# A pooling mixer computed on rounded high and low parts instead of plain fp32

## The chip, the cores and the metric

One core of one Trainium2 chip runs the whole network as one program. The metric is the device time of one execution in microseconds, of the slowest (here the only) core; lower is better.

## The reference, cut to what matters

The program is a stack of four mixers and feed-forward layers on 512 tokens of width 1024. The change touches the first mixer alone, a causal moving average minus the token itself, over four groups of 256 channels with windows of 2, 4, 8 and 16, followed by one 256 by 256 matrix for each group:

```python
h = rms_norm(x, norm_mix[0])
for g, win in enumerate((2, 4, 8, 16)):
    c = cs[:, :, g]                      # cumulative sum over tokens
    lag = jnp.pad(c[:, :-win], ((0, 0), (win, 0), (0, 0)))
    mean = (c - lag) / jnp.minimum(n_avail, float(win))[:, None]
    outs.append(mean - hf[:, :, g])
p = jnp.stack(outs, axis=2)
y = jnp.einsum('bsgc,gcd->bsgd', p, w).reshape(B, S, D)
x = x + y * scale
h = rms_norm(x, norm_ffn[0])             # then x = x + swiglu(h, ...)
```

## The kernel before

**How matrices are multiplied.** The network's accuracy is kept with two kinds of product on TensorE. Nearly everywhere an fp32 operand is split into a high part, rounded to the engine's fp32r format by a ScalarE copy, and a low part, the difference, taken by VectorE or GpSimd. `mm3` then multiplies high by high, high by low and low by high, three fp32r passes. `hilo` splits a tile, `hilo_g` (line 521) splits a tile times a per-partition gain, both with one ScalarE and one VectorE instruction. The pooling mixer alone uses plain fp32 matmuls, which the trace shows as two passes each.

**The pooling mixer** (`pool_mixer`, line 627). `x` is held transposed, channels on partitions, as eight tiles of 128 by 512. Because the pooling is linear, the group's matrix is applied first and the pooling after. `gains` multiplies the pool weights by the norm's gain. `squares` makes the sum of squares of the eight tiles of `x` (ScalarE squares, VectorE adds), has TensorE sum it over partitions (`col_sums`), and turns it into `rcol`, the reciprocal root mean square of each token (a VectorE step and a GpSimd power). `products` multiplies, for each group `g` and each half `jj` of the tokens, two token blocks `j` with two channel blocks `k` into one PSUM bank. `evac` reads that bank, multiplies by `rcol` and writes the tile `z`; a bank holds two halves of 256 columns, and each half has its own `rcol` column, so each half is an instruction of its own: ScalarE takes the first, VectorE the second. Then, for each of eight tiles `d`, `products` multiplies `z` by a banded matrix `bands[g]` (the moving average minus identity), and `finish` adds the result to `x` (VectorE), splits the new `x` into `xh` and `xl` (ScalarE, VectorE), squares it (ScalarE) and adds the square to `ss` (GpSimd).

**What follows.** The first feed-forward layer (`ffn`) starts each accumulation with `xh[0]`, `xl[0]` and goes to `xh[7]`, `xl[7]`; its TensorE queue runs on without a gap that matters. Its weights come through `Stream`: a raw tile of 2048 columns is loaded by SyncE's queue and split in four parts; `pump` issues one part (ScalarE's high part; the low part goes to VectorE and GpSimd in turn). The mixer's task `weights` pumps the first eight parts while the mixer runs.

**What sets the order.** Each engine works through its instructions in program order. The order is made while the kernel is built: tasks are generators, `Sched.run` steps the ready one with the lowest rank (then the one that has waited longest), and `Plan` keeps a price-based clock for each engine that says when a yielded tile will be there. `get` and `put` hand out PSUM banks: four named `acc`, two `t`, two `s`. The times of the plan fix nothing but the order. A tile's dependencies are turned into semaphore waits by the framework.

Of the kernel before, what the change touches and what calls it, by code (L numbers as in the profile page):

```python
# [9 lines left out]
F32R = mybir.dt.float32r  # L10
BF = mybir.dt.bfloat16
I32 = mybir.dt.int32
AF = mybir.ActivationFunctionType
OP = mybir.AluOpType
# [3 lines left out]
P = 128  # L18
# [3 lines left out]
KT = D // P  # L22
# [431 lines left out]
class Net:  # L454
# [37 lines left out]
    def mm(self, ps, lhsT, rhs, start=True, stop=True):  # L492
        self.nc.tensor.matmul(ps, lhsT, rhs, start=start, stop=stop)
# [133 lines left out]
    def pool_mixer(self):  # L627

        nc, a, sched = self.nc, self.a, self.sched
        self.ss = {}  # L630
        pw, bands, zs = [], [], {}
        for g in range(4):
            w = self.tmp("pw")
            nc.sync.dma_start(out=w, in_=a["pool_w"][:, g])
            nc.dma(0.73, w)
            pw.append(w)
            x = self.x[:, 2 * g:2 * g + 2]
            nc.sync.dma_start(out=x, in_=a["xT"][:, 2 * g:2 * g + 2])
            nc.dma(1.46, self.x[:, 2 * g], self.x[:, 2 * g + 1])
        for g in range(4):  # L640
            b = self.tmp("bnd")
            nc.sync.dma_start(out=b[:, :384], in_=a["bands"][:, g])
            nc.dma(0.55, b)
            bands.append(b)
        self.constants()
        self.ws.load()
        self.rcol = None
        self.new_norm("ffn0")

        def gains(g):  # L650
            yield pw[g]
            for k in range(2):
                c = slice(k * 256, (k + 1) * 256)
                nc.vector.tensor_scalar(pw[g][:, c], pw[g][:, c], self.vec("mix0", 2 * g + k),
                                        None, op0=OP.mult)

        def squares():
            for d in range(KT):
                yield self.x[:, d]
                q = self.tmp("sq")  # L660
                nc.scalar.activation(q, self.x[:, d], AF.Square)
                if d == 0:
                    self.ss["x"] = q
                else:
                    yield q
                    nc.vector.tensor_tensor(self.ss["x"], self.ss["x"], q, op=OP.add)
            ps = yield from self.get("t")
            yield self.ss["x"]
            self.col_sums("x", ps)
            self.rcol = False  # L670
            yield ps
            r = self.rstd(ps[:, :NT], D, "rcol")
            self.put("t")
            yield r
            self.rcol = r

        def evac(g, jj, tag, ps):
            while not self.rcol:
                yield 0.1
            yield ps  # L680
            z = self.tmp("z")
            for j in range(2):
                o = slice(j * 256, (j + 1) * 256)
                r = self.rcol[:, 2 * jj + j:2 * jj + j + 1]
                if j:
                    nc.vector.tensor_scalar(z[:, o], ps[:, o], r, None, op0=OP.mult)
                else:
                    nc.scalar.activation(z[:, o], ps[:, o], AF.Copy, scale=r)
            self.put(tag)
            yield z  # L690
            zs[g, jj] = z

        def finish(d, ps):
            nc.vector.scalar_tensor_tensor(self.x[:, d], ps, self.vec("pscale", d),
                                           self.x[:, d], op0=OP.mult, op1=OP.add)
            self.put("acc")
            yield self.x[:, d]
            self.xh[d], self.xl[d] = self.tmp("xh", F32R), self.tmp("xl", F32R)
            yield from self.split(self.xh[d], self.xl[d], self.x[:, d], self.vec("ffn0", d))
            self.square_sum("x", self.x[:, d], "x" not in self.ss, eng=nc.gpsimd)  # L700

        def products():
            for g in range(4):
                for jj in range(2):
                    tag = "acc" if g < 2 else "s" if g == 2 else "t"
                    if g == 2:
                        yield from self.wait("rcol")
                    ps = yield from self.get(tag)
                    yield pw[g], self.x[:, 2 * g], self.x[:, 2 * g + 1]
                    for j in (2 * jj, 2 * jj + 1):  # L710
                        for k in range(2):
                            self.mm(ps[:, (j % 2) * 256:(j % 2 + 1) * 256],
                                    self.x[:, 2 * g + k, j * P:(j + 1) * P],
                                    pw[g][:, k * 256:(k + 1) * 256], start=(k == 0),
                                    stop=(k == 1))
                    sched.spawn(evac(g, jj, tag, ps), 1, ps)
                    yield 0.0
            for d in range(KT):
                g, hd = d // 2, d % 2
                while (g, 0) not in zs or (g, 1) not in zs:  # L720
                    yield 0.1
                ps = yield from self.get("acc")
                yield bands[g]

                def mm(j, rhs, c0, c1, start=False, stop=False):
                    o = (j % 2) * 256 + hd * P
                    self.mm(ps[:, c0:c1], zs[g, j // 2][:, o:o + P], rhs, start, stop)

                b = bands[g]
                mm(0, b[:, 256:384], 0, 128, start=True)  # L730
                mm(0, b[:, 128:256], 128, 256)
                mm(2, b[:, 0:256], 256, 512)
                mm(1, b[:, 0:256], 128, 384)
                mm(3, b[:, 0:128], 384, 512, stop=True)
                sched.spawn(finish(d, ps), 1, ps)
                yield 0.0

        def weights():
            yield 14.0
            for i in range(8):  # L740
                self.ws.pump()
                yield 0.7

        for g in range(4):
            sched.spawn(gains(g), 0)
        sched.spawn(squares(), 1)
        sched.spawn(products(), 2)
        sched.spawn(weights(), 0)


# [1329 lines left out]
def _host(inp):  # L2080

    f = np.ascontiguousarray
    o = {}
# [33 lines left out]
    for name, w in (("mla_o", inp["mla_w_o"]), ("da_o", inp["da_w_out_2"])):  # L2117
        w = w[0].reshape(KT, P, 4, 2, P)
# [17 lines left out]
    r = np.arange(P)  # L2136
# [4 lines left out]
    c = np.arange(T)[None, :] - 3 * P - r[:, None]  # L2141
# [7 lines left out]
    o["causal"] = np.where(r[None, :] > r[:, None], np.float32(-1e30), np.float32(0))  # L2149

    o["ident"] = np.eye(P, dtype=np.float32)
    b = np.zeros((P, 4, 384), np.float32)
    p, c = np.arange(P)[:, None], np.arange(256)[None, :]
    for g, w in enumerate(WINDOWS):
        inside = (c - p >= 0) & (c - p < w)
        b[:, g, :256] = inside * np.float32(1.0 / w) - (c == p)
        n = np.minimum(c[:, :P] + 1, w).astype(np.float32)
        b[:, g, 256:] = inside[:, :P] / n - (c == p)[:, :P]
    o["bands"] = b
    return o  # L2160

# [38 lines left out]
```

## Time and profile before

| | us |
|---|---|
| median of three runs | 1568.91 |
| lowest, highest | 1567.87, 1570.69 |
| the profiled execution | 1568.89 |
| its span, first to last instruction | 1567.1 |

The span is what the profile's rows add up to; 1.79 us of the profiled execution lie outside it. PE is TensorE's matmul row and PEld its weight loads, DVE is VectorE, ACT ScalarE, POOL GpSimd. The mixer takes the first 42 us of the span, and the rest is the feed-forward layers, two attention mixers and a mixture of experts.

### The profile page before, as it was taken

How to read it: one execution, taken by the hardware profiler on the slowest of the kernel's cores; microseconds unless marked ns; L12 is line 12 of the kernel's file. 1: busy time of each engine (PE TensorE's matmuls, PEld its weight loads, DVE VectorE, ACT ScalarE, POOL GpSimd, SP SyncE). 2: the span in 40 equal slices, each digit the busy share in tenths (PEclk: the TensorE clock that was granted, in tenths of full speed). 3: DMA queues.
4: the chain of work that ended last, by engine and by line, in shares of the span. 5: the costliest groups of instructions: out<-in, count | busy, mean ns of one | idle time of the engine just before them, and what ended most of it. 6: DMA issues, size and time to landing. Idle time of an engine off the chain costs nothing. (4 is left out here: it accounts for less than half of the span.)

```text
span 1567.1 us, 21562 instructions
## 1 busy us (share of the span) xinstructions
PE 1495.6 (95%) x7752; PEld 1233.7 (79%) x7752; DVE 1017.4 (65%) x1668; ACT 782.9 (50%) x1585; POOL 508.8 (32%) x382
## 2 busy tenths in 40 slices
PE   8999999999999999999999999999989699999996
PEld 7788888888878888888888889998978466666664
DVE  6564344445477754443444466988984699999996
ACT  5323222323366633332233345787783478787884
POOL 4322122311231113321232223322222466565553
PEclk9999999999999999999999999999989699999998
DMA  6121333223210223214322232211068889999961
GB/s 241 61 107 56 116 111 108 73 75 119 69 63 28 68 108 121 99 42 142 108 86 86 74 119 84 78 55 68 28 202 296 261 302 362 345 355 360 348 206 27
DMA packets 69935, 221.61 MB, mean 141 GB/s; under 512 B 7616, under 2 KB 16960, under 8 KB 56640
## 3 DMA queue, kind: packets, MB, share of 16 engines
q1 hardware_dynamic: 56448, 201.03, 35.9%
q0 software_dynamic: 4064, 14.16, 3.7%
q10 hardware_dynamic: 9312, 5.01, 1.1%
q8 instruction: 62, 1.02, 0.3%
q14 instruction: 49, 0.40, 0.1%
HBM read 208.63 MB, written 11.53 MB: 140 GB/s over the span
## 5 line engine op out<-in xcount | busy, mean ns | idle before, releaser
L341 POOL TENSOR_TENSOR lo<-raw,hi 128x512 fp32r<-128x512 f32 (+1 forms) x157 | 224.4, 1439 | 694.4 <-ACT hi L341 592.4
L341 PE MATMUL acc<-xh,hi 128*128 128x512 f32 x744 | 290.5, 390 | 0.3 <-ACT xh L341 0.3
L341 PE MATMUL acc<-xl,hi 128*128 128x512 f32 x744 | 289.6, 389 | 0.3 <-DVE xl L341 0.3
L341 PE MATMUL acc<-xh,lo 128*128 128x512 f32 x744 | 289.5, 389 | 0.0
L341 DVE TENSOR_TENSOR wl<-raw,wh 128x512 fp32r<-128x512 f32 x288 | 268.1, 982 | 6.1 <-ACT wh L341 5.7
L341 ACT ACTIVATE hi<-raw 128x512 fp32r<-128x512 f32 (+1 forms) x378 | 208.8, 607 | 86.1 <-issue 59.8
L341 DVE TENSOR_TENSOR lo<-raw,hi 128x512 fp32r<-128x512 f32 (+1 forms) x221 | 215.9, 987 | 19.6 <-ACT hi L341 18.9
L341 ACT ACTIVATE wh<-raw 128x512 fp32r<-128x512 f32 x384 | 211.8, 621 | 15.8 <-PE acc L341 10.0
L341 POOL TENSOR_TENSOR wl<-raw,wh 128x512 fp32r<-128x512 f32 x96 | 147.1, 1533 | 119.4 <-ACT wh L341 90.8
L341 PEld LDWEIGHTS acc<-xh,hi 128*128 128x128 f32 x744 | 139.7, 188 | 29.6 <-ACT xh L341 0.7
L341 PEld LDWEIGHTS acc<-xl,hi 128*128 128x128 f32 x744 | 139.7, 188 | 29.1 <-DVE xl L341 0.6
L341 PEld LDWEIGHTS acc<-xh,lo 128*128 128x128 f32 x744 | 139.6, 188 | 29.1
L341 DVE TENSOR_TENSOR u<-acc,R 128x512 f32<-128x512 f32 x44 | 30.4, 691 | 181.0 <-PE acc L341 181.0
L341 PE MATMUL acc<-hh,hi 128*128 128x512 f32 x352 | 136.9, 389 | 0.0
L341 PE MATMUL acc<-hl,hi 128*128 128x512 f32 x352 | 136.9, 389 | 0.0
L341 PE MATMUL acc<-hh,lo 128*128 128x512 f32 x352 | 136.9, 389 | 0.0
L341 ACT ACTIVATE hh<-t 128x512 fp32r<-128x512 f32 x44 | 27.8, 632 | 218.4 <-DVE t L341 218.4
L341 DVE TENSOR_TENSOR x<-acc,x 128x512 f32<-128x512 f32 x59 | 40.5, 690 | 121.0 <-PE acc L341 120.9
L341 PE MATMUL acc<-hi,xh 128*128 128x256 f32 x384 | 111.0, 289 | 0.0
L341 PE MATMUL acc<-lo,xh 128*128 128x256 f32 x384 | 108.7, 283 | 0.6 <-DVE lo L341 0.6
L341 PE MATMUL acc<-hi,xl 128*128 128x256 f32 x384 | 108.5, 283 | 0.0
L341 PE MATMUL acc<-wl,teh 128*96 128x512 f32 x256 | 102.5, 401 | 3.3 <-POOL wl L341 1.7
(314 smaller groups left out, 2917.9 us busy)
## 6 DMA issues: line engine op xcount, KB each, us to landing
raw<-moe_w SPq DMA_DIRECT2D x200, 256.0 KB, 7.1
raw<-moe_w SPq DMA_DIRECT2D x46, 1024.0 KB, 7.3
raw<-ffn_gu SPq DMA_DIRECT2D x43, 1024.0 KB, 4.8
raw<-ffn_dn SPq DMA_DIRECT2D x32, 704.0 KB, 4.0
raw<-da_in SPq DMA_DIRECT2D x12, 1024.0 KB, 4.7
raw<-mla_up SPq DMA_DIRECT2D x4, 832.0 KB, 4.4
raw<-mla_o_a SPq DMA_DIRECT2D x12, 256.0 KB, 4.3
raw<-da_o_a SPq DMA_DIRECT2D x12, 256.0 KB, 3.9
```

What stands on the lines that cost most here:

```text
L341: r = f(*args, **kw)
```

## The change

`x` and the gained pool weights are split into high and low parts, and the products are made of three fp32r passes instead of two fp32 ones. `z` is split as it leaves PSUM, by `hilo_g`, half by half. The bands are loaded raw into `bndr` tiles (400 columns instead of 384) and rounded into fp32r tiles by GpSimd copies. The band of the first token block is stored as a high part and, for its first 16 columns, a low part; the other bands hold one fp32r value. Each `d` then takes nine fp32r matmuls instead of five fp32 ones: `z` high and low against the band, and one matmul of 16 columns for the band's low part. `squares` moves from rank 1 to rank 0 and follows the splits of `x`; `weights` waits for the sum of squares to have been issued instead of for a fixed time.

```diff
+        xs, ws, raws = [None] * KT, [None] * 4, []
...
         for g in range(4):
-            b = self.tmp("bnd")
-            nc.sync.dma_start(out=b[:, :384], in_=a["bands"][:, g])
-            nc.dma(0.55, b)
-            bands.append(b)
+            t = self.tmp("bndr")
+            nc.sync.dma_start(out=t[:, :400], in_=a["bands"][:, g])
+            nc.dma(0.57, t)
+            raws.append(t)
...
         def gains(g):
             yield pw[g]
+            h = self.pair("pw")
             for k in range(2):
                 c = slice(k * 256, (k + 1) * 256)
-                nc.vector.tensor_scalar(pw[g][:, c], pw[g][:, c], self.vec("mix0", 2 * g + k),
-                                        None, op0=OP.mult)
+                self.hilo_g(h[0][:, c], h[1][:, c], pw[g][:, c], self.vec("mix0", 2 * g + k))
+            yield h
+            ws[g] = h
+
+        def rounded():
+            yield from self.wait("rcol")
+            for t in raws:
+                yield t
+                b = self.tmp("bnd", F32R)
+                nc.gpsimd.tensor_copy(b[:, :400], t[:, :400])
+                yield b
+                bands.append(b)
+
+        def parts():
+            for d in range(KT):
+                yield self.x[:, d]
+                h = self.pair("xp")
+                self.hilo(*h, self.x[:, d])
+                xs[d] = h
 
         def squares():
             for d in range(KT):
-                yield self.x[:, d]
+                while xs[d] is None:
+                    yield 0.1
                 q = self.tmp("sq")
                 nc.scalar.activation(q, self.x[:, d], AF.Square)
...
-            z = self.tmp("z")
+            z = self.pair("z")
             for j in range(2):
                 o = slice(j * 256, (j + 1) * 256)
                 r = self.rcol[:, 2 * jj + j:2 * jj + j + 1]
-                if j:
-                    nc.vector.tensor_scalar(z[:, o], ps[:, o], r, None, op0=OP.mult)
-                else:
-                    nc.scalar.activation(z[:, o], ps[:, o], AF.Copy, scale=r)
+                self.hilo_g(z[0][:, o], z[1][:, o], ps[:, o], r)
             self.put(tag)
...
-                            self.mm(ps[:, (j % 2) * 256:(j % 2 + 1) * 256],
-                                    self.x[:, 2 * g + k, j * P:(j + 1) * P],
-                                    pw[g][:, k * 256:(k + 1) * 256], start=(k == 0),
-                                    stop=(k == 1))
+                            xh, xl = (t[:, j * P:(j + 1) * P] for t in xs[2 * g + k])
+                            wh, wl = (t[:, k * 256:(k + 1) * 256] for t in ws[g])
+                            self.mm3(ps[:, (j % 2) * 256:(j % 2 + 1) * 256], xh, xl, wh, wl,
+                                     k == 0, k == 1)
...
-                mm(0, b[:, 256:384], 0, 128, start=True)
-                mm(0, b[:, 128:256], 128, 256)
-                mm(2, b[:, 0:256], 256, 512)
-                mm(1, b[:, 0:256], 128, 384)
-                mm(3, b[:, 0:128], 384, 512, stop=True)
+                v = "p (a b) -> p a b"
+                for n in range(2):
+                    self.mm(ps[:, 0:256].rearrange(v, b=P), zs[g, 0][n][:, hd * P:(hd + 1) * P],
+                            b.rearrange(v, b=P)[:, 0:3:2], n == 0, False)
+                mm(0, 0, b[:, 384:400], 0, 16)
+                for j, c in ((2, 256), (1, 128)):
+                    for n in range(2):
+                        mm(j, n, b[:, 128:384], c, c + 256)
+                for n in range(2):
+                    mm(3, n, b[:, 128:256], 384, 512, stop=(n == 1))
                 sched.spawn(finish(d, ps), 1, ps)
                 yield 0.0
 
         def weights():
-            yield 14.0
+            yield from self.wait("rcol")
             for i in range(8):
                 self.ws.pump()
                 yield 0.7
...
-        sched.spawn(squares(), 1)
+        sched.spawn(parts(), 0)
+        sched.spawn(rounded(), 0)
+        sched.spawn(squares(), 0)
```

`_host` lays the bands out in the new order and makes the low part of the first block.

## Rows read from the trace of the kernel before

**Rows 1.** The page's first part: busy us, share of the span, instructions.

```profile
PE 1495.6 (95%) x7752; PEld 1233.7 (79%) x7752; DVE 1017.4 (65%) x1668; ACT 782.9 (50%) x1585; POOL 508.8 (32%) x382
```

**Rows 2.** Busy time by stretch, with the granted clock, DMA share and GB/s last.

```profile
10.00:15.00 5.00, 5.00 (x21) 4.28 (x20) 3.90 (x8) 2.30 (x4) 0.00 (x0) 1.00 1.07 365
...
30.00:35.00 5.00, 5.00 (x36) 4.69 (x36) 5.00 (x7) 4.28 (x8) 4.84 (x4) 1.00 0.64 234
...
60.00:70.00 10.00, 10.00 (x46) 8.29 (x45) 7.51 (x10) 3.35 (x6) 3.04 (x3) 1.00 0.37 123
```

**Rows 3.** Timeline of TensorE's matmuls: start, length, instruction, idle time before it.

```profile
6.49 9.67 PE L341 MATMUL acc<-pw,x 128*128 128x256 f32 x32 [6.49 <-DMA x<-xT]
15.99 0.95 PE L341 MATMUL pst<-ones,sq 128*128 128x1 f32 x8
...
23.79 12.43 PE L341 MATMUL acc<-bnd,z 128*128 128x128 f32 x80
...
42.10 0.50 PE L341 MATMUL acc<-xl,hi 128*128 128x512 f32 x1 [0.28 <-DVE xl L341]
...
43.26 1.05 PE L341 MATMUL pst<-ones,ss 128*128 128x1 f32 x8 [0.42 <-POOL ss L341]
```

**Rows 4.** Timeline of VectorE, 4 to 64 us.

```profile
4.78 0.62 DVE L341 TENSOR_SCALAR pw<-pw,vecs 128x256 f32<-128x256 f32 x2 [4.78 <-DMA vecs<-vecs]
...
11.86 3.87 DVE L341 TENSOR_TENSOR sq<-sq 128x512 f32<-128x512 f32 x5
...
22.36 0.48 DVE L341 TENSOR_SCALAR z<-pss,rcol 128x256 f32<-128x256 f32 x1 [2.62 <-ACT z L341]
...
27.02 0.73 DVE L341 SCALAR_TENSOR_TENSOR x<-acc,vecs,x 128x512 f32<-128x512 f32 x1
27.67 0.71 DVE L341 TENSOR_TENSOR lo<-raw,hi 128x512 fp32r<-128x512 f32 x1
...
41.30 0.75 DVE L341 SCALAR_TENSOR_TENSOR xl<-x,vecs,xh 128x512 fp32r<-128x512 f32 x1 [0.79 <-ACT xh L341]
```

**Rows 5.** Timeline of ScalarE, 4 to 64 us.

```profile
6.38 1.15 ACT L341 ACTIVATE sq<-x 128x512 f32<-128x512 f32 x2 [3.92 <-DMA x<-xT]
...
18.32 1.67 ACT L341 ACTIVATE hi<-raw 128x512 fp32r<-128x512 f32 x3 [4.60 <-DMA raw<-ffn_gu]
21.86 0.47 ACT L341 ACTIVATE z<-pss,rcol 128x256 f32<-128x256 f32 x1 [1.87 <-POOL rcol L341]
```

**Rows 6.** Timeline of GpSimd: the second sum of squares ends, its power follows.

```profile
41.93 1.27 POOL L341 TENSOR_TENSOR ss<-ss,sq 128x512 f32<-128x512 f32 x1 [0.93 <-ACT sq L341]
44.59 1.03 POOL L341 TENSOR_TENSOR rcol<-rcolv,mhalf 128x4 f32<-128x4 f32 x1 [1.39 <-DVE rcolv L341]
```

**Rows 7.** Timelines of ScalarE and VectorE in the second attention, one PSUM bank split.

```profile
979.01 0.84 ACT L341 ACTIVATE v<-acc,r 128x256 fp32r<-128x256 f32 x2
...
979.88 0.88 DVE L341 SCALAR_TENSOR_TENSOR v<-acc,r,v 128x256 fp32r<-128x256 f32 x2 [1.87 <-PE pss L341]
```

**Rows 8.** Groups by form, 0 to 45 us: count, busy us, mean ns, idle before.

```profile
L341 POOL TENSOR_TENSOR ss<-ss,sq 128x512 f32<-128x512 f32 x7 | 11.1, 1582 | 1.3 <-ACT sq L341 0.9
...
L341 DVE SCALAR_TENSOR_TENSOR xl<-x,vecs,xh 128x512 fp32r<-128x512 f32 x8 | 8.7, 1098 | 0.8 <-ACT xh L341 0.8
...
L341 DVE SCALAR_TENSOR_TENSOR x<-acc,vecs,x 128x512 f32<-128x512 f32 x8 | 5.9, 739 | 0.0
```

**Rows 9.** Timeline of TensorE: the first and the seventeenth of a run of 256-column fp32r matmuls.

```profile
961.79 0.28 PE L341 MATMUL acc<-hi,xh 128*128 128x256 f32 x1
...
963.71 0.28 PE L341 MATMUL acc<-hi,xl 128*128 128x256 f32 x1
```

**Rows 10.** Busy time by stretch around a gap in TensorE's work; the clock stands third from last.

```profile
1128.00:1131.00 3.00, 1.39 (x11) 0.87 (x8) 2.06 (x4) 2.91 (x7) 0.12 (x1) 1.00 0.00 0
1131.00:1132.00 1.00, 0.33 (x1) 0.18 (x1) 0.55 (x1) 0.97 (x3) 0.00 (x0) 0.58 0.00 0
1132.00:1138.00 6.00, 5.80 (x26) 5.80 (x27) 3.16 (x15) 2.92 (x12) 0.00 (x0) 0.50 0.00 0
```

More of the change, by code (lines that the diff above doesn't have):

```diff
@@ L708, in products @@
                     ps = yield from self.get(tag)
-                    yield pw[g], self.x[:, 2 * g], self.x[:, 2 * g + 1]
+                    while ws[g] is None or xs[2 * g + 1] is None:
+                        yield 0.1
+                    yield xs[2 * g] + xs[2 * g + 1]
                     for j in (2 * jj, 2 * jj + 1):
                         for k in range(2):
-                            self.mm(ps[:, (j % 2) * 256:(j % 2 + 1) * 256],
-                                    self.x[:, 2 * g + k, j * P:(j + 1) * P],
-                                    pw[g][:, k * 256:(k + 1) * 256], start=(k == 0),
-                                    stop=(k == 1))
+                            xh, xl = (t[:, j * P:(j + 1) * P] for t in xs[2 * g + k])
+                            wh, wl = (t[:, k * 256:(k + 1) * 256] for t in ws[g])
+                            self.mm3(ps[:, (j % 2) * 256:(j % 2 + 1) * 256], xh, xl, wh, wl,
+                                     k == 0, k == 1)
                     sched.spawn(evac(g, jj, tag, ps), 1, ps)
@@ L721, in products, with mm @@
                     yield 0.1
+                while len(bands) <= g:
+                    yield 0.1
                 ps = yield from self.get("acc")
                 yield bands[g]
-                def mm(j, rhs, c0, c1, start=False, stop=False):
+                def mm(j, n, rhs, c0, c1, start=False, stop=False):
                     o = (j % 2) * 256 + hd * P
-                    self.mm(ps[:, c0:c1], zs[g, j // 2][:, o:o + P], rhs, start, stop)
+                    self.mm(ps[:, c0:c1], zs[g, j // 2][n][:, o:o + P], rhs, start, stop)
                 b = bands[g]
-                mm(0, b[:, 256:384], 0, 128, start=True)
-                mm(0, b[:, 128:256], 128, 256)
-                mm(2, b[:, 0:256], 256, 512)
-                mm(1, b[:, 0:256], 128, 384)
-                mm(3, b[:, 0:128], 384, 512, stop=True)
+                v = "p (a b) -> p a b"
[8 more added lines that the diff above has]
+                    mm(3, n, b[:, 128:256], 384, 512, stop=(n == 1))
                 sched.spawn(finish(d, ps), 1, ps)
@@ L2151, in _host @@
     o["ident"] = np.eye(P, dtype=np.float32)
-    b = np.zeros((P, 4, 384), np.float32)
+    b = np.zeros((P, 4, 400), np.float32)
     p, c = np.arange(P)[:, None], np.arange(256)[None, :]
@@ L2155, in _host @@
         inside = (c - p >= 0) & (c - p < w)
-        b[:, g, :256] = inside * np.float32(1.0 / w) - (c == p)
+        b[:, g, 128:384] = inside * np.float32(1.0 / w) - (c == p)
         n = np.minimum(c[:, :P] + 1, w).astype(np.float32)
-        b[:, g, 256:] = inside[:, :P] / n - (c == p)[:, :P]
+        b[:, g, :128] = inside[:, :P] / n - (c == p)[:, :P]
+    high = (b[:, :, :128].view(np.uint32) & np.uint32(0xFFFFE000)).view(np.float32)
+    b[:, :, 384:] = (b[:, :, :128] - high)[:, :, :16]
+    b[:, :, :128] = high
     o["bands"] = b
```

## The prediction

> **What bounds the kernel now.** I read the page first. TensorE is busy for 1495.6 of 1567.1 us [rows 1], so over the whole span it is the bound, and a change that takes matmul passes away looks good. That is an average. The table of busy time by stretch, read next, tells another story of the 42 us that the change touches. Between 10 and 15 us TensorE works without a gap and VectorE 3.90 of 5 us; between 30 and 35 us VectorE is at 5.00 of 5 and TensorE as well; from 60 us on TensorE is full and VectorE is not [rows 2]. So the reader should ask which of the two ends the mixer last.
>
> TensorE's timeline answers: products from 6.49, the sums over partitions at 15.99 to 16.94, the bands from 23.79 to 36.22. The feed-forward layer starts right behind, but stops for its last input: the matmul at 42.10 waits 0.28 us for `xl` [rows 3]. VectorE's timeline shows that wait's other end, `xl` of tile 7, from 41.30 to 42.05 [rows 4]. From `rcol` at 21.86 [rows 5] to there VectorE hardly rests. **The end of the mixer is the end of VectorE's queue**, and TensorE, in front of its last three matmuls of the first group, merely waits. Behind it TensorE is full again [rows 2], so what the mixer loses or gains there the whole program does, one for one.
>
> VectorE's 42.05 us split into three parts. The sum of squares is ready at 11.86 + 3.87 = 15.73 [rows 4]; `rcol` follows at 21.82, because its steps stand in line behind weight parts that waited for their transfer (18.32, [rows 5]). The `z` tiles take from there to 27.02, when the first `x` step starts: 5.2 us. Then come eight `x` steps, eight `xl` and a weight part, to 42.05: 15.0 us [rows 4].
>
> **Part 1, up to `rcol`.** The order on each engine I worked out by stepping the tasks through the planner's rules; it gives ScalarE gains 0, copies of x0 and x1, squares 0 and 1, gains 1 and 2, and so on, and VectorE the same with the low parts and the adds. The durations come from rows. A VectorE instruction lasts 0.73 us and the next starts 0.65 us after it (27.02 and 27.67, [rows 4]), so 0.08 us overlap. One add or low part of 512 columns therefore costs about 0.61 us (0.69 long: 3.87 us for five, with small waits). A scaled low part of 256 columns costs 0.40 us (0.88 us for two of 0.48, [rows 7]); the plain multiply that it replaces cost 0.31 (0.62 for two, [rows 4]).
>
> x0 lands at 6.38 [rows 5]. Its copy takes some 0.61 us (1.67 for three with overlap, [rows 5]), so VectorE starts on x at about 7.0. It then has 8 low parts of x and 7 adds at 0.61 and 6 low parts of the weights at 0.40: 9.2 + 2.4 = 11.6 us, where it used to have 7 adds and 6 multiplies. Three waits for ScalarE early on add about 1.1 us. The sum of squares is then ready at 19.7, 4.0 us later than before. With no waits it is 18.6; both ends stay in the range.
>
> From that sum to `rcol` nothing stands in the way now, since `weights` follows it in program order. The second norm shows the bare chain: sum ready at 41.93 + 1.27 = 43.20, power from 44.59 to 45.62, 2.4 us [rows 6]. So `rcol` comes at 22.2 against 21.82: **+0.4 us**. The move of `weights` thus gives back most of what the splits cost. It costs nothing itself while ScalarE rounds the first three parts before `rcol` anyway, the raw tile landing at 18.3 [rows 5].
>
> The band copies by GpSimd stand ahead of its first weight part and of the power in its order, but need only transfers that land by about 13 us, when GpSimd is idle (0.00 of 5 us, [rows 2]). No row shows a 400-column copy; bounded by nothing below and by a 512-column two-input step of 1.58 us [rows 8] above, four end before 20 us at the worst. I take no cost. The 4% longer transfer of the bands lies behind `x` in SyncE's queue and is hidden likewise.
>
> **Part 2, the `z` tiles.** Before, a tile took one instruction of ScalarE and one of VectorE. Now each half takes both, and the second reads the first's result. There are two prices, far apart.
>
> If ScalarE may run ahead, VectorE's 16 low parts at 0.40, with three weight parts among them at 0.61, take 6.4 + 1.8 = 8.2 us instead of 5.2.
>
> But both halves of a tile lie in one PSUM bank, and the rows show what the program does with two readers of a bank. At 21.86 ScalarE reads the first half of `pss`, to 22.33; VectorE, which needs nothing from that instruction and has had `rcol` as long, starts on the other half at 22.36, and the wait is named as ScalarE's [rows 4, 5]. In the second attention ScalarE writes two halves `v` back to back from 979.01 to 979.85; VectorE, idle for 1.87 us, needs only the first, which ended at about 979.48, yet starts at 979.88, 0.03 us after the second [rows 7]. The later reader of a bank waits for the earlier one. No row has VectorE first and ScalarE second, but the wait is made from program order, and I see no reason that it should hold one way only. The new order inside a tile is ScalarE, VectorE, ScalarE, VectorE, all on one bank. So the second high part waits for the first low part, and the engines take turns.
>
> One tile then goes: high part 0 to 0.47, low part 0.50 to 0.98, high part 1.01 to 1.48, low part 1.51 to 1.99. The next tile's high part may follow 0.37 us after the second one (0.84 for two, [rows 7]), at 1.38, but its low part waits for VectorE until 1.92, so a tile costs 1.42 us. Seven tiles and a last one of 1.92 give 11.9 us. Three weight parts stand between them in ScalarE's order, each pushing the next high part by about 0.6: 13.7 us from `rcol` to the first `x` step. That is **+8.5 us** over 5.2. Queued behind on VectorE are the `x` steps, all of them, since the planner issues the tiles as one block; TensorE and the accumulation banks wait for these.
>
> The Trainium skill, "PSUM — Partial Sum Buffer", section "PSUM bank collisions raise a hardware error", says that any two engines on one bank have to be kept apart, reads against reads included, whatever columns they touch. By that the second price holds in either order of the engines; the rows here show one order.
>
> **Part 3, from the first `x` step to the last `xl`.** The work is the same: eight steps of 0.74 and eight of 1.10 us mean, slowed while GpSimd adds squares [rows 8]. The order differs: four `x` steps come at once, with four banks ready, so tile 7's is no longer last but one, and the wait of 0.79 us for its `xh` [rows 4] goes: **-0.8 us**. Together: 0.4 + 8.5 - 0.8 = 8.1 us.
>
> **TensorE's side.** A 256-column fp32r matmul follows the last after 0.12 us (1.92 us for 16, [rows 9]). Behind the sums there are 48 matmuls of products and 72 of bands; those of 128 and 16 columns no row shows, and I take them at 0.12 too (between nothing and that). With 1.0 us for the sums that is 15.4 us; before, the same stretch ran from 15.99 to 36.22, 20.2 us [rows 3]. The 4.8 us won go nowhere, because TensorE waits for VectorE: four bands can run before the first `x` step gives a bank back, then there are some 5 us without work.
>
> Such gaps have a price of their own. After 3 us with 1.39 us of work, the granted clock fell at 1131 to 0.50, the lower level of 1.2 GHz, and stayed there for 6 us of full work [rows 10]. At half rate the four bands still open take 4 x 9 x 0.24 = 8.6 us and the first feed-forward group up to tile 6 some 9.6, in 14 us that are there for both; it just fits if the clock comes back in six, as it did. I add nothing, and up to 3 us in the range. The Trainium skill, "TensorE: Matmul & The Clock Gate", names the same thing as a hazard of gaps between bursts; this trace agrees (0.50 after the gap at 1131).
>
> **The sum** is made against the profiled execution, 1568.89 us, which lies 0.02 us from the median: 1568.9 + 8.1 = 1577.0 us.
>
> **The rivals.** *The halves do not take turns* (ScalarE runs ahead). Then part 2 costs 8.2 - 5.2 = +3.0 and the sum is 0.4 + 3.0 - 0.8 = +2.6: 1571.5 us. For it: no row has ScalarE waiting. Against: the two rows where VectorE does.
> *TensorE is the bound.* It was without a gap from 6.49 to 36.2. If VectorE and ScalarE kept up, bands would end at 19.7 + 0.1 + 15.4 = 35.2 instead of 36.2 and the program would gain 1.0 us: 1567.9 us, not slower. It decides only if VectorE's queue ends before about 41 us. Even without turns it ends near 44.7, so I give it little.
> *The clock decides.* If it stays at the lower level from the gap until past the first group of 24 matmuls, TensorE ends bands and group at about 36 + 8.6 + 24 x 0.455 = 55.5 instead of 50.8, 4.7 us on top: 1581.7 us. For it: TensorE's work is thin from 30 to 45. Against: at half rate it is full there, and full work brought the clock back [rows 10].
>
> **How the numbers follow.** Turns: 0.68, its own range 1574 to 1580.5 us (sum ready earlier, copies overlapping better; against that a lower clock for a while). No turns: 0.15. TensorE the bound: 0.06. The clock: 0.11. The range from 1571.5 to 1581.5 leaves out the last two. About 0.2% (3.1 us) is what a measurement of this kernel can tell from no change. No turns and the TensorE case fall mostly within it: same 0.15. Faster keeps 0.05 for a price of part 1 that I have too high together with TensorE as the bound; slower has 0.80.
>
> **What the profile after would show.** Right: on `z`, ScalarE and VectorE alternate with starts some 0.5 us apart, and ScalarE's idle time there names VectorE; the first `x` step starts near 36 us, the last `xl` ends near 50; TensorE has gaps between 28 and 38 us. Wrong: ScalarE's second half of a tile starts before VectorE's first has ended; `rcol` later than 24 us (VectorE's splits dearer) or earlier than 20; the mixer's shift not found again at the end of the program, which would mean that a later stage gives or takes something.

## The result and the profile after

| | before | after |
|---|---|---|
| median of four runs, us | 1569.8 | 1584.03 |
| lowest, highest | 1567.87, 1571.66 | 1580.68, 1585.0 |
| profiled execution; its span | 1568.89; 1567.1 | 1585.0; 1583.2 |

The changed kernel is slower: ratio 1.0087, 95% interval 1.0067 to 1.0107. That is 14.2 us by the medians and 16.1 us between the two profiled executions, where 8.1 us had been forecast; 1584.0 lies above the range's upper end of 1581.5. The direction was right, and so was the largest of its three terms; the size was not.

The page's first part of the kernel after answers to [rows 1]:

```profile
PE 1497.7 (95%) x7776; PEld 1236.4 (78%) x7776; DVE 1030.9 (65%) x1684; ACT 793.2 (50%) x1609; POOL 506.5 (32%) x386
```

TensorE's busy time hardly moved, although two fp32 passes became three fp32r ones; the next views show that part of it ran at half the clock. VectorE has 13.5 us more to do. Neither says where 16 us went, so the mixer is read stage by stage. ScalarE's timeline after:

```profile
4.86 1.28 ACT L341 ACT_TABLE_LOAD   x1 [4.86 <-DMA pw<-pool_w]
...
9.04 1.69 ACT L341 ACTIVATE pwh<-pw,vecs 128x256 fp32r<-128x256 f32 x4
...
15.61 2.17 ACT L341 ACTIVATE sq<-x 128x512 f32<-128x512 f32 x4
...
26.79 0.48 ACT L341 ACTIVATE zh<-pss,rcol 128x256 fp32r<-128x256 f32 x1 [6.41 <-PE pss L341]
...
29.23 0.84 ACT L341 ACTIVATE zh<-acc,rcol 128x256 fp32r<-128x256 f32 x2 [0.58 <-DVE zl L341]
30.65 0.84 ACT L341 ACTIVATE zh<-acc,rcol 128x256 fp32r<-128x256 f32 x2 [0.58 <-DVE zl L341]
```

VectorE's timeline after, to be held against [rows 4]:

```profile
7.61 1.29 DVE L341 TENSOR_TENSOR xpl<-x,xph 128x512 fp32r<-128x512 f32 x2
9.57 1.69 DVE L341 SCALAR_TENSOR_TENSOR pwl<-pw,vecs,pwh 128x256 fp32r<-128x256 f32 x4 [0.67 <-ACT pwh L341]
...
12.50 2.21 DVE L341 TENSOR_TENSOR xpl<-x,xph 128x512 fp32r<-128x512 f32 x3
14.63 1.39 DVE L341 SCALAR_TENSOR_TENSOR pwl<-pw,vecs,pwh 128x256 fp32r<-128x256 f32 x2
15.95 1.00 DVE L341 TENSOR_TENSOR sq<-sq 128x512 f32<-128x512 f32 x1
...
18.08 3.86 DVE L341 TENSOR_TENSOR sq<-sq 128x512 f32<-128x512 f32 x5
...
24.04 0.69 DVE L341 TENSOR_TENSOR lo<-raw,hi 128x512 fp32r<-128x512 f32 x1
...
29.74 0.88 DVE L341 SCALAR_TENSOR_TENSOR zl<-acc,rcol,zh 128x256 fp32r<-128x256 f32 x2 [0.54 <-ACT zh L341]
31.16 0.88 DVE L341 SCALAR_TENSOR_TENSOR zl<-acc,rcol,zh 128x256 fp32r<-128x256 f32 x2 [0.54 <-ACT zh L341]
...
39.35 0.48 DVE L341 SCALAR_TENSOR_TENSOR zl<-pst,rcol,zh 128x256 fp32r<-128x256 f32 x1 [0.54 <-ACT zh L341]
39.75 2.35 DVE L341 TENSOR_TENSOR lo<-raw,hi 128x512 fp32r<-128x512 f32 x2
42.03 2.71 DVE L341 SCALAR_TENSOR_TENSOR x<-acc,vecs,x 128x512 f32<-128x512 f32 x4
...
47.02 0.75 DVE L341 SCALAR_TENSOR_TENSOR x<-acc,vecs,x 128x512 f32<-128x512 f32 x1 [0.30 <-PE acc L341]
...
51.38 6.90 DVE L341 SCALAR_TENSOR_TENSOR xl<-x,vecs,xh 128x512 fp32r<-128x512 f32 x4
```

The turns are there as forecast. `zh` waits 0.58 us for `zl`, `zl` waits 0.54 us for `zh`, and pairs of one tile's second and the next tile's first half start 1.42 us apart (29.23, 30.65; 29.74, 31.16). The sum of squares is ready at 18.08 + 3.86 = 21.94, the first `z` starts at 26.79, the first `x` step at 42.03, and the last `xl` ends at 51.38 + 6.90 = 58.28.

The turns could also come from the tile in SBUF that both engines use, since ScalarE would write the second half of `zh` while VectorE reads the first. The splits of the weights speak against that. `hilo_g` makes them in the same order, half by half, but reads SBUF and not PSUM, and there the engines take no turns: four high parts run through from 9.04 (1.69 us, some 0.4 apart), the second already under way when VectorE starts on the first at 9.57, and the four low parts follow each other just as closely. So the turns go with the bank.

GpSimd's timeline after; then TensorE's, with the starts of products at two paces:

```profile
13.64 2.77 POOL L341 CAST bnd<-bndr 128x400 fp32r<-128x400 f32 x4 [12.76 <-DMA bndr<-bands]
24.27 1.37 POOL L341 TENSOR_TENSOR rcol<-rcolv,mhalf 128x4 f32<-128x4 f32 x1 [7.86 <-DVE rcolv L341]
...
39.91 3.33 POOL L341 TENSOR_TENSOR lo<-raw,hi 128x512 fp32r<-128x512 f32 x2 [3.68 <-ACT hi L341]
46.52 11.20 POOL L341 TENSOR_TENSOR ss<-ss,sq 128x512 f32<-128x512 f32 x7 [3.29 <-ACT sq L341]
```

```profile
16.17 0.28 PE L341 MATMUL acc<-pwh,xpl 128*128 128x256 f32 x1
22.09 1.83 PE L341 MATMUL pst<-ones,sq 128*128 128x1 f32 x8 [5.63 <-DVE sq L341]
...
24.36 0.41 PE L341 MATMUL pss<-pwh,xpl 128*128 128x256 f32 x1
24.57 0.41 PE L341 MATMUL pss<-pwh,xph 128*128 128x256 f32 x1
...
27.69 0.28 PE L341 MATMUL pss<-pwl,xph 128*128 128x256 f32 x1
27.81 0.28 PE L341 MATMUL pss<-pwh,xpl 128*128 128x256 f32 x1
...
42.91 0.55 PE L341 MATMUL acc<-bnd,zh 128*128 128x256 f32 x1 [6.10 <-DVE x L341]
```

Busy time by stretch after; the granted clock stands third from last:

```profile
15.00:20.00 5.00, 1.45 (x13) 1.25 (x11) 4.79 (x8) 4.07 (x9) 1.41 (x3) 1.00 0.95 387
20.00:21.00 1.00, 0.00 (x0) 0.00 (x0) 0.90 (x2) 0.38 (x1) 0.00 (x0) 0.75 1.01 426
21.00:27.00 6.00, 4.91 (x23) 4.95 (x24) 1.61 (x4) 0.21 (x1) 2.62 (x2) 0.50 0.30 126
27.00:30.00 3.00, 3.00 (x26) 3.00 (x26) 1.62 (x4) 1.87 (x5) 0.00 (x0) 0.95 0.02 5
...
41.00:48.00 7.00, 5.09 (x24) 5.12 (x25) 6.70 (x10) 5.20 (x9) 3.63 (x4) 0.51 0.45 150
```

TensorE has two gaps, not one: 5.63 us ahead of the sums and 6.10 us ahead of the fifth band. Behind each the clock stands at 0.50, the level of 1.2 GHz, for some six us. At that level 256-column matmuls follow each other in 0.21 us (24.36, 24.57), at full clock in 0.12 (27.69, 27.81), and the eight sums last 1.83 us instead of 0.95 [rows 3].

Against before, the first `z` comes 26.79 - 21.86 = 4.9 us later, the phase from there to the first `x` step is 15.24 instead of 5.16 us (+10.1), and that from there to the end of the last `xl` 16.25 instead of 15.03 (+1.2). Together +16.2. What is left of the span behind the last `xl` is 1524.9 us after and 1525.05 before. The whole loss is made in the mixer and passed on one for one.

### The profile page after: what moved, and what is told of

Read it like the earlier page. It is cut to its first block, busy times and chain, and to the rows that moved or that the text cites. A ratio compares the mean times of both kernels' runs of the same rounds, so it can differ in the third digit from the quotient of the medians.

```text
span 1583.2 us, 21658 instructions
## 1 busy us (share of the span) xinstructions
PE 1497.7 (95%) x7776; PEld 1236.4 (78%) x7776; DVE 1030.9 (65%) x1684; ACT 793.2 (50%) x1609; POOL 506.5 (32%) x386
## 5 line engine op out<-in xcount | busy, mean ns | idle before, releaser
L341 POOL TENSOR_TENSOR wl<-raw,wh 128x512 fp32r<-128x512 f32 x96 | 142.2, 1482 | 124.8 <-ACT wh L341 94.1
L341 PE MATMUL acc<-wh,teh 128*96 128x512 f32 x256 | 106.0, 414 | 0.0
```

Source lines behind the costliest of these rows:

```text
L341: r = f(*args, **kw)
```

## The experiments

One table holds the mixer's stages of every profiled kernel, read from its timelines as above (us from the span's start). "z phase" runs from the first `z` instruction to the first `x` step, "x phase" from there to the end of the last `xl`. Behind it the profiled executions need between 1521.6 and 1525.6 us more, with no order that the mixer explains, and the runs of one kernel lie 2.5 to 8.5 us apart. The transfers scatter too: the first pool weights let ScalarE start at 4.86 us after, at 4.81 in e1, 4.49 in e2 and 4.32 in e4. A difference of half a microsecond in the first three columns can be theirs. So for a single mend of 1 or 2 us the end of the mixer is the sharper measure, and the time ratio is given beside it.

| kernel | squares summed | first z | z phase | x phase | last xl ends | time / before, 95% interval |
|---|---|---|---|---|---|---|
| before | 15.73 | 21.86 | 5.16 | 15.03 | 42.05 | 1 |
| after | 21.94 | 26.79 | 15.24 | 16.25 | 58.28 | 1.0087 (1.0067 to 1.0107) |
| e1 both high parts first | 21.93 | 26.78 | 11.02 | 16.23 | 54.03 | 1.0083 (1.0069 to 1.0096) |
| e2 products earlier | 21.57 | 24.66 | 16.31 | 16.24 | 57.21 | 1.0094 (1.0079 to 1.0110) |
| e3 table load first | 21.57 | 26.42 | 15.24 | 16.26 | 57.92 | 1.0090 (1.0076 to 1.0104) |
| e4 products' part alone | 20.39 | 25.25 | 6.74 | 16.42 | 48.41 | 1.0047 (1.0033 to 1.0060) |
| e5 sums on VectorE | 21.84 | 26.70 | 15.25 | 14.25 | 56.20 | 1.0077 (1.0062 to 1.0093) |
| e6 bands' part alone | 16.25 | 19.38 | 14.01 | 16.03 | 49.42 | 1.0041 (1.0026 to 1.0056) |
| e7 e1, e2, e3 and e5 | 21.82 | 24.75 | 12.20 | 14.26 | 51.21 | 1.0059 (1.0046 to 1.0073) |
| e8 before, weights later | 15.65 | 19.23 | 6.17 | 19.51 | 44.91 | 1.0031 (1.0020 to 1.0043) |
| e9 e6 with e1 and e5 | 16.20 | 19.28 | 9.91 | 14.85 | 44.04 | 1.0008 (0.9998 to 1.0018) |
| e10 before, sums on VectorE | 15.70 | 21.55 | 5.16 | 15.25 | 41.96 | 0.9990 (0.9981 to 1.0000) |
| e11 e8 with e10 | 15.67 | 18.80 | 6.64 | 17.09 | 42.53 | 1.0005 (0.9994 to 1.0016) |

**e1: both high parts of a tile ahead of both low parts.**

```diff
-            for j in range(2):
...
-                self.hilo_g(z[0][:, o], z[1][:, o], ps[:, o], r)
+            for o, r in cuts:
+                nc.scalar.activation(z[0][:, o], ps[:, o], AF.Copy, scale=r)
+            for o, r in cuts:
+                nc.vector.scalar_tensor_tensor(z[1][:, o], ps[:, o], r,
+                                               z[0][:, o].bitcast(F32), op0=OP.mult,
+                                               op1=OP.subtract)
```

> In each z tile both high parts are issued ahead of both low parts; nothing else differs from the changed kernel. Turns theory (a PSUM bank's later reader waits for its earlier one, so the two engines alternate): a tile falls from 1.42 us to 2 x 0.40 = 0.80 us, the first x step comes some 5 us earlier than 42.0 and the time falls by about 5 us from 1584.0, to 1579. Rival, the extra VectorE work itself or TensorE's low clock sets the end: the tiles get shorter, but the last xl still ends near 58 us and the time stays within 1 us.

VectorE's timeline of e1:

```profile
28.51 3.22 DVE L341 SCALAR_TENSOR_TENSOR zl<-acc,rcol,zh 128x256 fp32r<-128x256 f32 x8
31.65 1.33 DVE L341 TENSOR_TENSOR lo<-raw,hi 128x512 fp32r<-128x512 f32 x1
```

Eight low parts in 3.22 us with no wait: 0.80 us a tile instead of 1.42. The arithmetic is that of the change, only the order on the bank differs. The mixer ends 4.25 us earlier, so the turns are shown to be a cost of the order. The median (1581.37, on another chip) lies 2.7 us below that of the kernel after, which is less than the mixer's end says and within what runs differ by.

**e2: group 2's products ahead of the sums.**

```diff
-                    if g == 2:
+                    if g == 3:
                         yield from self.wait("rcol")
```

> The products of group 2 no longer wait in program order for the sums over partitions, so TensorE has 24 matmuls to do in its gap from 16.5 to 22.1 us. Clock theory: the granted clock stays at 1.0 into the sums, these take about 1.0 us instead of 1.83, the first z no longer waits for its products, and it starts near 24.8 us instead of 26.8; the time falls by about 2 us. Rival, part 1 is late by VectorE's splits alone: the first z starts less than 0.7 us earlier and the time stays.

ScalarE's first `z` of e2, and VectorE's step behind the last `zl`:

```profile
24.66 0.47 ACT L341 ACTIVATE zh<-pss,rcol 128x256 fp32r<-128x256 f32 x1 [5.48 <-POOL rcol L341]
```

```profile
37.01 4.03 DVE L341 TENSOR_TENSOR lo<-raw,hi 128x512 fp32r<-128x512 f32 x3
```

The first `z` no longer waits for `pss` but for `rcol`, and comes 2.1 us earlier. Of that, 0.37 us is the earlier sum of squares, whose weights had landed sooner; the rest had been TensorE's. Its gap ahead of the sums is shorter but not closed (3.24 us), and the eight sums last 1.19 us instead of 1.83. Order and clock changed together here, so the run does not tell the two apart. Half of the 2.1 us is lost again, since three weight parts instead of two now stand ahead of the `x` steps, 1.3 us each, beside three of GpSimd's. The end gains 1.07 us; the time shows nothing.

**e3: the activation table loaded ahead of the first split** (a ScalarE copy of a constant at the start).

```diff
+        warm = c.tile([P, 1], F32, name="warm")
+        nc.scalar.activation(warm, self.ones, AF.Copy)
```

> A one-column copy of a constant is put ahead of everything on ScalarE, so its table load no longer stands behind the wait for the first pool weights. Theory: the load runs near 1.2 us instead of 4.86 us, the first scaled weights start near 4.9 us instead of 6.15 us, and the sum of squares is ready 0.6 to 1.2 us earlier than 21.9 us; the time falls by about as much, which is less than the time itself can tell. Rival, VectorE waits for x anyway: the sum of squares is ready at 21.9 us as before.

Before, the load of 1.28 us ran at 1.17 us while nothing had landed; after, it stands behind the wait for `pool_w` at 4.86, and in e3 it runs at 1.18. The first low part of `x` starts at 6.92 us instead of 7.61. At the sum of squares 0.37 us of that is left, and 0.36 at the mixer's end, less than the 0.6 to 1.2 expected. But e2, without this edit, has its sum of squares at the same 21.57, because its weights landed earlier. So a gain at the end is not shown.

**e4 and e6: each half of the change alone.** e4 splits `x` and the weights and makes fp32r products, and keeps fp32 `z` and bands. e6 keeps fp32 products and splits `z` and rounds the bands. Both move `weights`. The cuts are shown against the kernel after.

```diff
 # e4
-            z = self.pair("z")
+            z = self.tmp("z")
...
 # e6
-                            self.mm3(ps[:, (j % 2) * 256:(j % 2 + 1) * 256], xh, xl, wh, wl,
-                                     k == 0, k == 1)
+                            self.mm(ps[:, (j % 2) * 256:(j % 2 + 1) * 256],
+                                    self.x[:, 2 * g + k, j * P:(j + 1) * P],
+                                    pw[g][:, k * 256:(k + 1) * 256], start=(k == 0),
+                                    stop=(k == 1))
```

> Only the products are made from rounded parts; z is one plain fp32 tile, and the bands are plain fp32, both as before the change. If part 1 (splits of x and of the weights, table load, low clock) costs some 5 us and the turns in z the rest: the first z starts near 26 us, the first x step some 5 us later, the last xl ends near 47 us, and the time is 1574 to 1576 us, 4 to 6 above the kernel before. Rival, the turns are the whole loss: within 1.5 us of the kernel before.

> Only z and the bands are made from rounded parts; the products stay plain fp32 as before the change, and the squares come in the new rank. If z's turns cost what the trace shows: the clock stays at 1.0 up to the sums, the first z starts at 18.5 to 20 us, the first x step comes 14 to 15 us later, and the last xl ends at 49 to 51 us, 7 to 9 us later than before: 1577 to 1579 us. Rival, part 1 (splits of x, clock) carries the loss: last xl within 3 us of 42.05.

Each half loses by itself: the mixer ends 6.4 us later with the products' part, 7.4 with the bands'. (In e4 that is 1.4 us more than expected; the time of e6, 1574.57 us, rose less than expected.) In e6, where TensorE's gap ahead of the sums is 0.78 us and the clock stays at 1.00 there, `z` starts 2.5 us earlier than before and the z phase is the long one. In e4 the z phase is only 1.6 us longer than before, and the first `z` comes 3.4 us late.

Both together lose 16.2 us, 2.5 more than the sum. By stages the surplus lies at the first `z`: 3.4 later and 2.5 earlier make 0.9, and both together are 4.9 late. Two parts of these 4.0 us are known. Both halves hold the move of `weights`, which by e8 brings the first `z` forward by 2.6 us, so it counts twice in the sum; and the band copies stand beside VectorE's splits only in the whole change, 1.1 us as the next rows show. The later phases are together 1.5 us shorter than the sum; why is not shown. In e4, which has no band copies, VectorE's timeline reads:

```profile
12.12 1.89 DVE L341 TENSOR_TENSOR xpl<-x,xph 128x512 fp32r<-128x512 f32 x3
13.93 0.88 DVE L341 SCALAR_TENSOR_TENSOR pwl<-pw,vecs,pwh 128x256 fp32r<-128x256 f32 x2
14.72 0.69 DVE L341 TENSOR_TENSOR sq<-sq 128x512 f32<-128x512 f32 x1
```

The same steps last 2.21, 1.39 and 1.00 us in the kernel after, while GpSimd copies bands (13.64 to 16.41): 1.1 us more in all.

**e5: the adds of squares in the `x` steps on VectorE instead of GpSimd.**

```diff
-            self.square_sum("x", self.x[:, d], "x" not in self.ss, eng=nc.gpsimd)
+            self.square_sum("x", self.x[:, d], "x" not in self.ss, eng=nc.vector)
```

> The changed kernel with the seven adds of the second sum of squares on VectorE instead of GpSimd. Theory, xl is slow because VectorE and GpSimd hold each other up on SBUF: each xl takes 0.74 us (not up to 1.7), the x phase is 8 x 0.66 + 8 x 0.66 + 7 x 0.61 = 14.8 us instead of 16.25, so the extra adds on VectorE cost less than the hold-up did, and the last xl or add ends 1 to 1.5 us earlier than 58.3. Rival, xl is long by itself in this order: it stays above 1 us and the phase grows by 4 us.

VectorE's timeline of e5, from the stretch where four `xl` lasted 6.90 us after:

```profile
52.94 0.73 DVE L341 SCALAR_TENSOR_TENSOR xl<-x,vecs,xh 128x512 fp32r<-128x512 f32 x1
53.60 0.67 DVE L341 TENSOR_TENSOR ss<-ss,sq 128x512 f32<-128x512 f32 x1
54.20 0.73 DVE L341 SCALAR_TENSOR_TENSOR xl<-x,vecs,xh 128x512 fp32r<-128x512 f32 x1
```

An `xl` and an add together last 1.26 us, less than one `xl` did beside GpSimd (1.7). VectorE does seven adds more, and the x phase is 2.0 us shorter.

**e7: e1, e2, e3 and e5 together.**

> The changed kernel with z's high parts ahead of its low parts, the products of group 2 ahead of the sums, the early table load, and the second sum's adds on VectorE. From the trace of each alone (mixer's end 4.2, 1.1 and 0.4 us earlier, and 1.4 hoped for) the last xl should end near 51 us, and the time should be about 1577 us, still 7 above the kernel before. Rival, the mends overlap, since each only moves the wait to the next engine: last xl later than 54 us.

The mixer ends 7.1 us earlier than after, and still 9.2 us later than before; mixer's end (51.21) and time (1577.52) came out as expected. The squares are summed 6.1 us later than before, with all the splits on VectorE ahead of them, and three weight parts ahead of the first `x` step last 4.92 us.

**e8: the kernel before with its weight parts behind the power.** The change has them a step earlier, behind the sums over partitions.

```diff
-            yield 14.0
+            while not self.rcol:
+                yield 0.2
```

> The kernel before, with one part of the change: the task of the weights waits, here until the power has been issued. Theory, rcol was late before only by weight parts standing ahead of it: the power starts near 17.5 us instead of 20.77, the first z near 18.6 instead of 21.9, the first x step 1 to 2 us earlier than 27.0 (TensorE's bands start at 23.8 either way), the last xl 1 to 2 us earlier than 42.05, and the time is 1567 to 1569 us. Rival, TensorE holds the first x step where it was: last xl within 0.5 us of 42.05.

The first `x` step came 1.6 us earlier, but the mixer ended 2.9 us later and the kernel was slower. VectorE's timeline of e8:

```profile
29.91 1.59 DVE L341 SCALAR_TENSOR_TENSOR xl<-x,vecs,xh 128x512 fp32r<-128x512 f32 x1
31.43 1.76 DVE L341 TENSOR_TENSOR lo<-raw,hi 128x512 fp32r<-128x512 f32 x1
...
35.45 1.65 DVE L341 SCALAR_TENSOR_TENSOR xl<-x,vecs,xh 128x512 fp32r<-128x512 f32 x1
```

Weight parts moved into the x phase, where VectorE's steps stand beside GpSimd's adds and weight parts, and they slowed: an `xl` from 1.10 to 1.6, a `lo` from 0.7 to 1.76. This run refuted my view of the move as a plain gift.

**e9: e6 with the edits of e1 and e5.**

> The bands' part alone (x and weights unsplit, fp32 products as before; z in pairs, bands rounded), with both high parts of a z tile ahead of both low parts, and the adds of squares in the x steps on VectorE. Theory (turns and hold-up with GpSimd are what the bands' part lost): first z at 19.4 us as with the bands alone, z phase 14.0 - 4.3 = 9.7 us, x phase 14.3 instead of 16.0, last xl at 43.4, so 6.0 us less than the bands alone and 1.3 us behind the kernel before: 1570.2 us. Rival (the clock decides: TensorE, behind a gap of some 4 us, can't feed the x steps in time at its lower level): VectorE's steps then wait for acc, and the last xl ends at 46 us or later, 1573 us.

VectorE's timeline of e9, and its busy time by stretch:

```profile
20.21 3.23 DVE L341 SCALAR_TENSOR_TENSOR zl<-acc,rcol,zh 128x256 fp32r<-128x256 f32 x8 [0.63 <-ACT zh L341]
...
43.31 0.73 DVE L341 SCALAR_TENSOR_TENSOR xl<-x,vecs,xh 128x512 fp32r<-128x512 f32 x1
```

```profile
25.00:30.00 5.00, 3.53 (x31) 3.38 (x29) 5.00 (x10) 3.37 (x9) 3.00 (x3) 1.00 0.55 193
```

The last `xl` ends at 44.04, 5.4 us earlier than in e6 (6.0 expected), and the time is that of before within 0.2%. TensorE's gap there is 1.55 us, not the rival's 4, and the clock stays at 1.00: the rival did not happen.

**e10 and e11: the kernels before and e8 with the adds on VectorE.** The edit is that of e5.

> The kernel before with one edit, the adds of squares in the x steps on VectorE instead of GpSimd. Theory (GpSimd's two-input adds and VectorE's two-input steps hold each other up): every xl falls from 1.10 us mean to 0.74, 8 x 0.36 = 2.9 us, against 7 adds at 0.61 = 4.3 us; the x phase goes from 15.0 to at most 16.4 us and, with the weight part held up no longer, more likely 14.9: last xl between 41.5 and 43.5, 1568.4 to 1570.4 us, no change that can be measured. Rival (xl lasts 1.1 us by itself, or from ScalarE): VectorE has 4.3 us more to do, x phase 19.3, last xl at 46.3, 1573 us.

> The kernel before with the weights' splits behind the power (as in e8) and the adds of squares in the x steps on VectorE (as in e10). Theory (in e8 the weight parts were dear only because they and the xl stood beside GpSimd's adds): the first x step stays at 25.4 us, lo last 0.7 and xl 0.73, the x phase falls from 19.5 to about 16.5 us (15.3 of e10 and two more weight parts at 0.61), last xl at 41.9, where TensorE's fp32 bands, whose end hardly moves, leave it: no change against the kernel before, 1567.3 to 1569.5 us, and 1% of e8's loss or 0.3% given back. Rival (weight parts on VectorE between the x steps cost by themselves, or TensorE's clock falls at 45 as in e8 for another reason): x phase 18 or more, last xl at 43.5 or later, 1571 us or more.

In e10 VectorE has seven adds more and its x phase is 0.2 us longer, not 4.3: seven of eight `xl` last 0.73 or 0.74 us. The one that does not (29.97) starts beside a weight part of GpSimd's (28.80 to 30.53). The `xl` of 28.65 started 0.15 us ahead of that part and kept its 0.74; there the part paid, with 1.73 us instead of 1.27. VectorE's timeline of e10:

```profile
28.65 0.74 DVE L341 SCALAR_TENSOR_TENSOR xl<-x,vecs,xh 128x512 fp32r<-128x512 f32 x1
29.31 0.74 DVE L341 SCALAR_TENSOR_TENSOR x<-acc,vecs,x 128x512 f32<-128x512 f32 x1
29.97 1.11 DVE L341 SCALAR_TENSOR_TENSOR xl<-x,vecs,xh 128x512 fp32r<-128x512 f32 x1
31.00 0.68 DVE L341 TENSOR_TENSOR ss<-ss,sq 128x512 f32<-128x512 f32 x1
```

e11 takes 2.4 us off e8's x phase, which ends at 42.53. The clock from 45 to 50 us is 1.00, where it was 0.50 in e8, and the loss of e8 is gone (the two intervals don't meet). So it was GpSimd's adds that made e8's order dear; without them the x phase is still 2.1 us longer than before, and the earlier start of `z` makes up for all but 0.5 us of it. No run was faster than the kernel before by more than 0.2%; e10 comes nearest.

## Why the prediction was wrong in its size

Its three terms were +0.4, +8.5 and -0.8. They measured +4.9, +10.1 and +1.2. The missing 8.1 us are 4.5, 1.6 and 2.0. Of the signs named beforehand, the alternation on `z` came, and the mixer's shift was found whole at the end of the program. But `rcol` came at 24.27 + 1.37 = 25.64, later than the 24 us that were to mean dearer splits, and the first `x` step and the last `xl` came 6 and 8 us behind the places named (36 and 50).

**Part 1 failed, +0.4 us for `rcol`.** Two of its steps did not hold. "The sum of squares is then ready at 19.7": it was 21.94, 2.2 us later. VectorE came to `x` at 7.61 instead of 7.0, since ScalarE first loaded its table and scaled weights (0.6). The band copies, of which I wrote "I take no cost", ended before 20 us as bounded, but they stood beside VectorE's splits: 1.39, 1.00 and 2.21 us for steps that last 0.88, 0.69 and 1.89 in e4, 1.1 us in all. An add was priced at 0.61 us, and the 3.87 us for five were put down to "small waits". After, all squares were made by 15.61 + 2.17 = 17.78, and the five adds from 18.08 on still took 3.86: where each adds to the sum of the one before, they start 0.79 us apart (0.8 in all). Waits for ScalarE took 0.7 us where 1.1 was allowed. That makes 2.1 of the 2.2 us.

"The bare chain" of 2.4 us to `rcol` was 3.7, and the first `z` came 1.15 us behind it: the sums lasted 1.83 at half clock instead of 0.95 (1.05 in the second norm), the power 1.37 instead of 1.03 [rows 6] beside a weight part on VectorE (24.04), and `z` of group 2 waited for products that stand behind the sums and ran at half clock too. The forecast's own 19.7 + 2.4 = 22.1 us (its 22.2 is 0.1 too high) lies 0.2 behind the first `z` of before, and 0.2 + 2.2 + 1.3 + 1.15 = 4.9. In the kernel before, the power that ends at 21.82 reads:

```profile
20.77 1.05 POOL L341 TENSOR_TENSOR rcol<-rcolv,mhalf 128x4 f32<-128x4 f32 x1
```

**"I add nothing" for the clock failed at a place that I had not looked at.** I worked out the gap behind the bands and forgot the one in front of the sums: if products are faster and the splits later, TensorE is done at 16.45 and idle until 22.09. The clock fell there, on the path to `rcol` and `z`: 0.9 us at the sums, and all of the 1.15 at `z` by this estimate: sums of 0.95 from 22.09 and twelve products at 0.12 would have ended near 24.5, ahead of the power. No run changed the clock alone. The gap that I did foresee (36.8 to 42.9) also lowered the clock, but one `x` step alone waited for it, 0.30 us (47.02). The clock rival as I put it, at the end of the bands, did not happen. That the clock comes back was read from [rows 10], which end while it is at 0.50; the next stretch of that trace, 1138 to 1139 us, has it at 1.00.

**Part 2 held, +8.5 us for the turns.** The tiles took 13.0 us from the first high part to the end of the last low part, where 11.9 and two weight parts at 0.6 make 13.1. The rest, 1.6 us, is a weight part more between the last tile and the first `x` step, and both of these slowed beside GpSimd's: 2.35 us for two. e1 confirms the cause by taking it away. The rival without turns is refuted for this order, and so is TensorE as the bound: its gaps are waits for VectorE.

The Trainium skill, "PSUM — Partial Sum Buffer", section "PSUM bank collisions raise a hardware error", says that two engines must be kept from using one bank in the same partitions at the same time, two reads too. The program's waits follow it in both orders now: ScalarE waits for VectorE's read here (0.58 us), VectorE for ScalarE's in [rows 4].

**Part 3 had the wrong sign, -0.8 us.** The wait for tile 7's `xh` went, as forecast. But I took the mean of 1.10 us for an `xl` as a property of the step. It is one of what runs beside it. After, four `xl` in a row stood beside adds all the way, 1.7 us each. With no add on GpSimd every `xl` lasts 0.73 or 0.74 (e5, e9), and the phase is 14.25 us in e5.

The Trainium skill, "SBUF — State Buffer", section "Who interferes with whom", says that a VectorE instruction with two SBUF inputs contends with a GpSimd instruction that reads SBUF, and one with a single SBUF input, outside the two-port modes, does not. The traces agree: `xl` (0.73 to 1.7 us), `lo` (0.7 to 1.76) and the adds (0.69 to 1.00) slow down, while `x`, whose other input lies in PSUM, lasts 0.74 us wherever it stands.

**"The move of `weights` gives back most of what the splits cost"** held for the start of `z` (e6: 19.38 instead of 21.86) and failed for the end: the parts come back in the z and x phases, at up to 1.76 us (e8).

## What to carry to other kernels

When a producer for VectorE or ScalarE is made of two dependent reads of one PSUM bank, issue all reads of the first engine before those of the second; the same arithmetic cost 1.42 or 0.80 us a tile. Before costing a two-input VectorE step by its mean, look at what GpSimd does in the same microseconds; taking GpSimd's adds over to VectorE made its x phase 2.0 us shorter in e5 and 0.2 longer in e10. And when TensorE's work gets shorter in front of a wait, ask which matmuls stand right behind the gap, for here these ran at the lower clock, and the first `z` waited for them.

## What the runs showed of the hardware

- GpSimd and VectorE slow each other: beside `xl` GpSimd's adds take 1.6 us each (seven in 11.20) and the `xl` 1.7; apart, 1.27 us [rows 6] and 0.73. The pair takes less than one after the other would (2.0), so it is not a full turn each.
- A GpSimd power of four columns lasts 1.37 us in all seven kernels where a weight part on VectorE stands beside it (after, e1 to e5, e7), and 1.05 or less in the six where none does.
- A GpSimd copy of 128 by 400 fp32 into fp32r takes 0.52 us where VectorE reads PSUM (the last one in e9, at 20.66) and 0.69 in the mean beside VectorE's splits (four in 2.77), which it slows in turn: 1.1 us in all.
- The first fp32r products of the kernel after, from 8.73 us on, also follow each other in 0.21 us, and in 0.12 only from 13.8, though the profile's granted clock is 1.00 from 5 to 15 us. What held them is open.
